# Seven multiplications instead of eight for some block products of the MLP, with groups of 1,024 columns

## The chip, the core and the metric

The kernel runs on one core of one Trainium2 chip. The metric is the device time of one execution in microseconds (us); before the change the median of 3 runs is 1461.17 us (1460.38 to 1461.81).

## What is computed

The reference is one layer of a decoder trunk on 256 tokens of width 2048, in float32. Three token mixers (softmax attention, gated linear attention, spatial gating) read one input projection, their outputs are merged by gates and projected by `w_o`; then comes the MLP, which is the part that the change touches:

```python
h = x + merged @ w_o
hn = rms_norm(h, n2)
return h + jnp.square(jax.nn.relu(hn @ w1)) @ w2     # w1: 2048 x 8192, w2: 8192 x 2048
```

## The kernel before

Every weight matrix is streamed from HBM once. A product in float32 is made of three matmuls: an operand is split into a rounded high part (type F32R) and the rest, and activation-high x weight-high, activation-high x weight-low and activation-low x weight-high are added up in PSUM. The activations are the stationary operand: `xT`, `yT`, `mT`, `hT` and `fT` hold them transposed, 16 k-tiles of 128 rows, high parts of the 256 tokens first, then the low parts. The weights are the moving operand.

`group_a` (L211) computes 512 output columns for both halves of the tokens (two PSUM banks, `ga`). It takes the weights in pieces from `weights` (L193): `fetch` (L170) brings 4 k-tiles x 512 columns, 1 MB, into `wraw` by one DMA on the SP queue (3 buffers); `split_w` (L182) makes the parts of two k-tiles, `whi` by a copy on ScalarE (L189) and `wlo` by a subtraction on VectorE (L190), 3 buffers each; `products` (L200) runs the 12 matmuls of such a piece (L207 to L209). After each piece `step` (L135) runs one waiting piece of other work, put there by `later` (L132).

The MLP goes through four phases `ph` of 2048 inner columns. In each, four groups with `w_ff1` on `hT` (L705) are followed by four with `w_ff2` on `fT` (L715). After a `w_ff1` group ScalarE applies ReLU and square (L708, L709) into `ft`, and `turn_into` (L649) turns `ft` back into `fT`: 4 transposes on TensorE into a bank `tt`, a copy on ScalarE for the high part, a subtraction on VectorE for the low one. One such step is called a turn here; there are two per 512 columns. After a `w_ff2` group VectorE adds the bank, scaled, to `h` (L718). `hT` is made the same way while `w_o` runs (L682 to L695), and its last two turns fall into the first group of the MLP. VectorE adds the `w_o` banks to `h` (L686) and ScalarE sums the squares of it (L688).

The order of the instructions is left to a scheduler, except for the first group of the kernel, where `tc.manual_schedule` keeps the written order on TensorE, ScalarE, VectorE and SP. Each engine works its own list in order.

Of the kernel before, what the change touches and what calls it, by code (L numbers as in the profile page):

```python
# [11 lines left out]
F32 = mybir.dt.float32  # L12
# [45 lines left out]
def trunk(ctx: ExitStack, tc: tile.TileContext, x, rpe_table, norm1_g, w_in, q_norm_g, k_norm_g,  # L58
# [24 lines left out]
    rows2 = cpool.tile([NV, P], F32, name="rows2")  # L83
# [4 lines left out]
    rpe = cpool.tile([NB, NH], F32, name="rpe")  # L88
    nc.gpsimd.dma_start(rpe, rpe_table)
    oneh = cpool.tile([NB, T], F32, name="oneh")  # L90
    nc.gpsimd.dma_start(oneh, onehot)
    lrwb = cpool.tile([LR + 1, 512], F32, name="lrwb")
    nc.gpsimd.dma_start(lrwb[:LR, :], gla_lr_w[0])
    nc.gpsimd.dma_start(lrwb[LR:LR + 1, :], gla_lr_b)
    og = cpool.tile([P, DV], F32, name="og")
    nc.gpsimd.dma_start(og, gla_out_g.to_broadcast([P, DV]))
    lng = cpool.tile([P, 512], F32, name="lng")
    nc.gpsimd.dma_start(lng, sg_ln_g.to_broadcast([P, 512]))
    lnb = cpool.tile([P, 512], F32, name="lnb")
    nc.gpsimd.dma_start(lnb, sg_ln_b.to_broadcast([P, 512]))  # L100
    sgw = cpool.tile([P, NH, P], F32, name="sgw")
    nc.gpsimd.dma_start(sgw, sg_w[0].rearrange("g t s -> t g s"))


    def tri(name, op, pat, cm):
        t = cpool.tile([P, P], F32, name=name)
# [10 lines left out]
    cum_r = cpool.tile([P, P], F32R, name="cum_r")  # L117
    nc.gpsimd.tensor_copy(cum_r, cum)
    rest_r = cpool.tile([P, P], F32R, name="rest_r")
    nc.gpsimd.tensor_copy(rest_r, rest)  # L120
    cind = cpool.tile([P, 2], F32, name="cind")
    nc.gpsimd.memset(cind, 0.0)
    nc.gpsimd.memset(cind[0:CH, 0:1], 1.0)
    nc.gpsimd.memset(cind[CH:P, 1:2], 1.0)
# [2 lines left out]
    def v3(t, a):  # L127
        return t.rearrange("p (a b) -> p a b", a=a)
# [116 lines left out]
    rb = gpool.tile([NB, NH, P], F32, name="rb")  # L245

    def first_group(c0):

# [43 lines left out]

    def squares(c):
        for tt in range(NT):
            junk = gpool.tile([P, XC], F32, tag="junk", name="junk")
# [109 lines left out]


    lrs = gpool.tile([P, NT, LR], F32, name="lrs")
    lrT = gpool.tile([LR + 1, T], F32, name="lrT")
    nc.vector.memset(lrT, 1.0)
    dec = gpool.tile([P, NT, NH, 2], F32, name="dec")  # L410
    G16 = 1.0 / 16.0
# [42 lines left out]
    wT = gpool.tile([P, NH, P], F32, name="wT")  # L454
    nc.gpsimd.memset(wT, 0.0)

    def w_turn():
# [130 lines left out]
    def outputs(hp, tt):  # L588
        if tt == 0:
            ob[hp] = v3(t4("ob"), NT)  # L590
        ps = bank("po")
        for j in range(2):
            hh = 2 * hp + j
            o = ps[:, j * DV:(j + 1) * DV]
            mm(o, am[:, tt, hh, :], vb[hp][:, tt, j * DV:(j + 1) * DV], start=True, stop=False, skip_group_check=True)  # L595
            for cc in range(2):
                c = 2 * tt + cc
                if c:
                    s = st[hp, 2] if c == 3 else st[hp, 0][:, c - 1, :]
                    mm(o[cc * CH:(cc + 1) * CH, :], qdT[:, hh, c * CH:(c + 1) * CH], s[:, j * DV:(j + 1) * DV],  # L600
                       start=False, stop=True, skip_group_check=True)
        nc.scalar.activation(ob[hp][:, tt, :], ps, AF.Copy)
        for j in range(2):
            junk = gpool.tile([P, XC], F32, tag="junk", name="junk")
# [49 lines left out]
    mg = None  # L654
    for n in range(D // 512):
        gts = []
        for i in range(3):
            pg = group_a(w_in[0], 0, KT, C_GATE + i * D + n * 512, 512, xT)
            if mg is None:
                drain()  # L660
                br_ctx.__exit__(None, None, None)
                mg = ctx.enter_context(tc.tile_pool(name="mg", bufs=1))
# [17 lines left out]
    hT = acts.tile([P, KT, 2 * T], F32R, tag="act0", name="hT")  # L680
    hsq = gpool.tile([P, NT, 4], F32, name="hsq")
    for n in range(D // 512):  # L682
        po = group_a(w_o[0], 0, KT, n * 512, 512, mT)
        for tt in range(NT):
            hv = h[:, tt, n * 512:(n + 1) * 512]
            nc.vector.tensor_add(hv, po[tt], hv)  # L686
            junk = gpool.tile([P, XC], F32, tag="junk", name="junk")
            nc.scalar.activation(junk, hv, AF.Square, accum_out=hsq[:, tt, n:n + 1])  # L688
        later()
        for jp in range(2):  # L690
            k = n * 4 + 2 * jp
            srcs = [h[:, tt, (k + j) * P:(k + j + 1) * P] for j in range(2) for tt in range(NT)]
            later(lambda k=k, srcs=srcs: turn_into(hT, k, srcs, V_N2))

    r2 = gpool.tile([P, NT], F32, name="r2")  # L695
    hs = gpool.tile([P, NT], F32, name="hs")
# [2 lines left out]
    nc.vector.reciprocal(r2, hs)  # L699


    fT = acts.tile([P, KT, 2 * T], F32R, tag="act1", name="fT")
    for ph in range(FF // D):
        for g in range(D // 512):
            pz = group_a(w_ff1[0], 0, KT, ph * D + g * 512, 512, hT)  # L705
            ft = mg.tile([P, NT, 512], F32, tag="ft", name="ft", bufs=2)
            for tt in range(NT):
                nc.scalar.activation(ft[:, tt, :], pz[tt], AF.Relu)  # L708
                nc.scalar.activation(ft[:, tt, :], ft[:, tt, :], AF.Square)  # L709
            later()  # L710
            for jp in range(2):
                srcs = [ft[:, tt, (2 * jp + j) * P:(2 * jp + j + 1) * P] for j in range(2) for tt in range(NT)]
                later(lambda k=g * 4 + 2 * jp, srcs=srcs: turn_into(fT, k, srcs, None))
        for n in range(D // 512):
            pf = group_a(w_ff2[0], ph * D, KT, n * 512, 512, fT)  # L715
            for tt in range(NT):
                hv = h[:, tt, n * 512:(n + 1) * 512]
                nc.vector.scalar_tensor_tensor(hv, pf[tt], r2[:, tt:tt + 1], hv, op0=ALU.mult, op1=ALU.add)  # L718
                if ph == FF // D - 1:
                    nc.sync.dma_start(out[0, tt * P:(tt + 1) * P, n * 512:(n + 1) * 512], hv)  # L720


# [20 lines left out]
```

## Time and profile before

| | us |
|---|---|
| median of 3 runs | 1461.17 |
| profiled execution | 1461.76 |
| its span | 1459.9 |
| TensorE busy | 1449.0 (99%) |
| VectorE busy | 758.7 (52%) |
| ScalarE busy | 685.1 (47%) |
| share of the 16 DMA engines, weight queue | 57.1% |

PE is TensorE's matmul row, PEld its weight load, DVE VectorE, ACT ScalarE, SP the queue that issues the DMAs. Matmuls are pipelined, so the time of one is read from the distance of two starts, not from its duration. The MLP runs from 743.07 us to the end.

### The profile page before, as it was taken

The numbers are of one execution on the slowest core, as the hardware profiler recorded it, in microseconds if no ns is written. First come the engines' busy times: TensorE is split into PE (matmuls) and PEld (weight loads), VectorE is DVE, ScalarE is ACT, GpSimd is POOL, SyncE is SP. The second block draws the span as 40 slices with busy tenths as digits, with TensorE's granted clock in tenths as the row PEclk, the third lists the DMA queues.
The fourth block names the chain that finished last, engine by engine and source line by source line (L and its number), as shares of the span: only waits on it lengthen the run. The fifth ranks groups of instructions, "written<-read, shape, count | busy, mean of one in ns | idle before, by whom it ended". The sixth has DMA issues, their size and how long they took to land.

```text
span 1459.9 us, 16296 instructions
## 1 busy us (share of the span) xinstructions
PE 1449.0 (99%) x6608; PEld 1197.8 (82%) x6608; DVE 758.7 (52%) x822; ACT 685.1 (47%) x821; POOL 14.0 (1%) x37
## 2 busy tenths in 40 slices
PE   8999999999999999999999999999999999999998
PEld 6899887788888888888888888888888888888887
DVE  5654655454645546465555455544544455554454
ACT  6457444454444444444545544445334554345432
POOL 2000000000000000000000000000000000000000
PEclk9999999999999999999999999999999999999999
DMA  8555554545655555555556555655556555666563
GB/s 281 185 183 163 182 177 137 181 155 191 201 180 195 195 185 196 193 185 183 188 173 187 188 188 189 199 177 198 181 194 201 175 193 182 200 189 186 181 222 115
DMA packets 138810, 272.19 MB, mean 186 GB/s; under 512 B 4748, under 2 KB 11440, under 8 KB 138736
## 3 DMA queue, kind: packets, MB, share of 16 engines
q1 hardware_dynamic: 137808, 268.59, 57.1%
q0 software_dynamic: 928, 2.57, 0.5%
q8 instruction: 51, 0.84, 0.2%
q14 instruction: 23, 0.19, 0.0%
HBM read 268.26 MB, written 2.88 MB: 186 GB/s over the span
## 4 chain that ended last, share of the span: by engine, by line
PE 99%; DMA 0%; SPq 0%; DVE 0%; issue 0%
PE ga L207 32%; PE ga L209 32%; PE ga L208 31%; PE tt L221 1%; PE pst L576 0%; DMA h<-in_x_dram 0%; PE po L600 0%; PE po L595 0%; PE qkt L221 0%; PE xt L221 0%; PE psc L364 0%; PE pbias L317 0%; PE pz L425 0%; PE pmx L465 0%; PE pam L557 0%; PE ybt L221 0%
## 5 line engine op out<-in xcount | busy, mean ns | idle before, releaser
L190 DVE TENSOR_TENSOR wlo<-wraw,whi 128x1024 fp32r<-128x1024 f32 (+3 forms) x520 | 619.2, 1193 | 644.3 <-ACT whi L189 644.1
L189 ACT ACTIVATE whi<-wraw 128x1024 fp32r<-128x1024 f32 (+3 forms) x520 | 537.8, 1036 | 720.8 <-PE ga L209 713.3
L207 PE MATMUL ga<-whi,xT 128*128 128x512 f32 (+2 forms) x768 | 297.8, 388 | 0.0
L208 PE MATMUL ga<-wlo,xT 128*128 128x512 f32 (+2 forms) x768 | 293.5, 382 | 0.0
L209 PE MATMUL ga<-whi,xT 128*128 128x512 f32 (+2 forms) x768 | 293.5, 382 | 0.0
L207 PE MATMUL ga<-whi,hT 128*128 128x512 f32 x512 | 201.7, 394 | 0.0
L207 PE MATMUL ga<-whi,fT 128*128 128x512 f32 x512 | 199.9, 391 | 0.0
L209 PE MATMUL ga<-whi,hT 128*128 128x512 f32 x512 | 199.5, 390 | 0.0
L209 PE MATMUL ga<-whi,fT 128*128 128x512 f32 x512 | 199.3, 389 | 0.0
L208 PE MATMUL ga<-wlo,fT 128*128 128x512 f32 x512 | 199.2, 389 | 0.0
L208 PE MATMUL ga<-wlo,hT 128*128 128x512 f32 x512 | 199.1, 389 | 0.0
L207 PEld LDWEIGHTS ga<-whi,xT 128*128 128x128 f32 x768 | 144.9, 189 | 29.8 <-issue 3.9
L209 PEld LDWEIGHTS ga<-whi,xT 128*128 128x128 f32 x768 | 144.7, 188 | 26.8
L208 PEld LDWEIGHTS ga<-wlo,xT 128*128 128x128 f32 x768 | 144.9, 189 | 25.2
L209 PEld LDWEIGHTS ga<-whi,hT 128*128 128x128 f32 x512 | 96.1, 188 | 20.3
L209 PEld LDWEIGHTS ga<-whi,fT 128*128 128x128 f32 x512 | 96.1, 188 | 20.0
L208 PEld LDWEIGHTS ga<-wlo,fT 128*128 128x128 f32 x512 | 96.2, 188 | 19.8
L207 PEld LDWEIGHTS ga<-whi,fT 128*128 128x128 f32 x512 | 96.1, 188 | 19.5
L208 PEld LDWEIGHTS ga<-wlo,hT 128*128 128x128 f32 x512 | 96.3, 188 | 19.2
L207 PEld LDWEIGHTS ga<-whi,hT 128*128 128x128 f32 x512 | 96.2, 188 | 19.0
L207 PE MATMUL ga<-whi,mT 128*128 128x512 f32 x128 | 51.4, 402 | 0.0
L209 PE MATMUL ga<-whi,mT 128*128 128x512 f32 x128 | 50.7, 396 | 0.0
(217 smaller groups left out, 825.0 us busy)
## 6 DMA issues: line engine op xcount, KB each, us to landing
wraw<-in_w_ff_dram SPq DMA_DIRECT2D x128, 1024.0 KB, 5.2
wraw<-in_w_in_dram SPq DMA_DIRECT2D x80, 1024.0 KB, 5.0
wraw<-in_w_o_dram SPq DMA_DIRECT2D x16, 1024.0 KB, 5.1
wraw<-in_w_br_b_dram SPq DMA_DIRECT2D x8, 1024.0 KB, 5.2
wraw<-in_w_in_dram SPq DMA_DIRECT2D x8, 692.0 KB, 4.1
wraw<-in_w_br_a_dram SPq DMA_DIRECT2D x4, 1024.0 KB, 5.2
wraw<-in_w_br_c_dram SPq DMA_DIRECT2D x4, 1024.0 KB, 5.1
wraw<-in_w_in_dram SPq DMA_DIRECT2D x6, 512.0 KB, 11.5
```

Source lines behind the costliest of these rows:

```text
L189: nc.scalar.activation(hi[:, j:j + per, :w], src, AF.Copy)
L190: nc.vector.tensor_tensor(lo[:, j:j + per, :w], src, hi[:, j:j + per, :w].bitcast(F32), ALU.subtract)
L207: mm(ps[tt][:, :w], xh, hi[:, j, :w], start=(k == 0), stop=False)
L208: mm(ps[tt][:, :w], xh, lo[:, j, :w], start=False, stop=False)
L209: mm(ps[tt][:, :w], xl, hi[:, j, :w], start=False, stop=(k == nk - 1))
L221: nc.tensor.transpose(ps[:, i * P:(i + 1) * P], s, ident)
```

## The change

The MLP now works in groups of 1,024 columns and takes the 16 k-tiles in 8 pairs. A pair of k-tiles, two halves of the tokens and two halves of the columns make a 2x2 block product. Five of the eight pairs ("P" in `ORDER = "PPSPSPSP"`) are computed with eight block multiplications as before (24 matmuls). The other three ("S") use a scheme with seven (21 matmuls): four sums of the weight blocks are formed on VectorE (`fsum`, L803 to L805), four sums of the activation blocks when the activations are turned (`sums`, L673 to L679), and at the end of a group the extra banks P1, P5, P6 and P7 are combined (`seven`, L831). An S pair is run as two pieces, "A" (3 products) and "B" (4). With the four output banks a group holds all 8 PSUM banks.

The weight pool, the gate pool and some small tiles now lie in memory that is given up before the MLP; the MLP's tiles (`fT`, `fraw`, `fhi`, `flo`, `fsum`, `fu`) lie in a pool of their own that is opened after the last `w_o` group. The whole MLP is written in a fixed order on TensorE, ScalarE, VectorE and SP: the parts of piece i+2 are prepared before the matmuls of piece i (`LEAD = 2`, three buffers), and the DMAs run two pairs ahead. L numbers in the diff's new functions are those of the changed kernel.

```diff
+ORDER = "PPSPSPSP"
+SEVEN = [i for i, c in enumerate(ORDER) if c == "S"]
...
-    def turn_into(dst, k, srcs, gain):
+    def turn_into(dst, k, srcs, gain, sums=None):
         ps = bank("tt")
         transpose4(ps, srcs)
-        split_ps(dst[:, k:k + 2, :], v3(ps, 2), None if gain is None else cols[:, gain + k:gain + k + 2])
+        if sums is not None:
+            a = scratch[-1].tile([P, 2, T], F32, tag="a32", name="a32")
+            if gain is None:
+                nc.scalar.activation(a, v3(ps, 2), AF.Copy)
...
+        split_ps(dst[:, k:k + 2, :], src, None if gain is None else cols[:, gain + k:gain + k + 2])
+        if sums is None:
+            return
+        b = src.rearrange("p j (t c) -> p (j t) c", c=P)
+        s = scratch[-1].tile([P, 4, P], F32, tag="s32", name="s32")
+        nc.vector.tensor_tensor(s[:, 0:2, :], b[:, 0:2, :], b[:, 1:4:2, :], ALU.subtract)
+        nc.vector.tensor_tensor(s[:, 2, :], s[:, 1, :], b[:, 0, :], ALU.subtract)
+        nc.vector.tensor_tensor(s[:, 3, :], s[:, 2, :], b[:, 2, :], ALU.add)
+        nc.scalar.activation(sums[:, 0], s, AF.Copy)
+        nc.vector.tensor_tensor(sums[:, 1], s, sums[:, 0].bitcast(F32), ALU.subtract)
...
+    mg_ctx.__exit__(None, None, None)
+    w_ctx.__exit__(None, None, None)
+    ffp = ctx.enter_context(tc.tile_pool(name="ffp", bufs=1, reuse_waits="tile"))
...
+    def prep(piece, raws):
+        g, what, kp, q = piece
+        raw = raws[q]
+        hi, lo = parts()
+        if what == "P":
+            split2(hi, lo, 0, 4, raw, 2 if q == 0 else 4)
+        elif what == "A":
+            ts = ffp.tile([P, 4, GW], F32, tag="fsum", name="fsum")
+            raws[q] = raw, ts
+            nc.vector.tensor_tensor(ts[:, 0:2], raw[:, 1:3], raw[:, 0:1].to_broadcast([P, 2, GW]), ALU.add)
+            nc.vector.tensor_add(ts[:, 2], ts[:, 0], raw[:, 2])
+            nc.vector.tensor_add(ts[:, 3], ts[:, 2], raw[:, 3])
+            split2(hi, lo, 0, 3, raw[:, 1:4])
+        else:
+            raw, ts = raws.pop(q)
+            split2(hi, lo, 0, 4, ts, 2)
+        return hi, lo
...
+            if what == "A":
+                todo = (("P1", block(g, kp, 0, 0)), ("c12", kind(g, kp, 3)), ("c11", block(g, kp, 0, 1)))
+            else:
+                todo = (("P5", kind(g, kp, 1)), ("P7", kind(g, kp, 0)), ("P6", kind(g, kp, 2)),
+                        ("c21", block(g, kp, 1, 1)))
+            for i, (role, a) in enumerate(todo):
+                g.three(role, *a, hi[:, i], lo[:, i])
+    def seven(g):
+        b = g.banks
+        u = ffp.tile([P, 4, GW], F32, tag="fu", name="fu")
+        nc.scalar.activation(u[:, 1], b["P1"], AF.Copy)
+        nc.vector.tensor_add(u[:, 0], u[:, 1], b["P6"])
+        nc.vector.tensor_add(u[:, 3], u[:, 0], b["P7"])
+        nc.vector.tensor_sub(u[:, 0], b["P5"], u[:, 0])
+        nc.vector.tensor_sub(u[:, 2], b["P5"], u[:, 3])
+        return u
...
+            nc.vector.tensor_add(u[:, 1], u[:, 1], b["c11"])
+            nc.vector.tensor_add(u[:, 3], u[:, 3], b["c21"])
+            nc.vector.tensor_add(u[:, 0], u[:, 0], b["c12"])
+            nc.vector.tensor_add(u[:, 2], u[:, 2], b["c22"])
+            for i in (1, 3, 0, 2):
+                nc.scalar.activation(u[:, i], u[:, i], AF.Relu)
+                nc.scalar.activation(u[:, i], u[:, i], AF.Square)
...
+    with tc.manual_schedule(engines=ORDERED):
+        for i in range(LEAD):
+            ready(i)
+        for i, piece in enumerate(pieces):
+            g = piece[0]
+            ends = i + 1 == len(pieces) or pieces[i + 1][0] is not g
+            if ends:
+                g.first(g)
+            ready(i + LEAD)
+            multiply(piece, wts.pop(i), half=turns.pop(0) if turns and len(turns) == 1 else None)
+            if len(turns) == 2:
+                turns.pop(0)()
+            step()
+            if ends:
+                turns = g.last(g)
```

`g.first` is `seven`, followed in a `w_ff2` group by four scaled additions into `h` (L869); `g.last` is the ReLU and square shown above (`w_ff1`) or four more such additions (`w_ff2`). A group of `w_ff1` leaves four turns, two after the first piece of the next group and two inside the second.

Two places of the order matter below. The first is VectorE after the end of a `w_ff1` group. Before, it goes on with weight parts (`wlo`) and two low parts of `fT`:

```order
L190 TENSOR_TENSOR wlo<-wraw,whi 128x1024 x7
L161 TENSOR_TENSOR fT<-tt,fT 128x2x256
L190 TENSOR_TENSOR wlo<-wraw,whi 128x1024
L161 TENSOR_TENSOR fT<-tt,fT 128x2x256
L190 TENSOR_TENSOR wlo<-wraw,whi 128x1024 x7
```

Now, after the end of the first `w_ff1` group (`flo` is the low part of a piece: 1536 wide for A, twice 1024 for B, 2048 for P; `a_5829`, `s_5833` and `sums` belong to a turn that also makes sums):

```order
L791 TENSOR_TENSOR flo<-fraw,fhi 128x1536
L166 TENSOR_TENSOR fT<-a_5829,fT 128x2x256
L675 TENSOR_TENSOR s_5833<-a_5829 128x256
L676 TENSOR_TENSOR s_5833<-s_5833,a_5829 128x128
L677 TENSOR_TENSOR s_5833<-s_5833,a_5829 128x128
L679 TENSOR_TENSOR sums<-s_5833,sums 128x512
L166 TENSOR_TENSOR fT<-tt,fT 128x2x256
L791 TENSOR_TENSOR flo<-fsum,fhi 128x1024 x2
L166 TENSOR_TENSOR fT<-tt,fT 128x2x256 x2
L791 TENSOR_TENSOR flo<-fraw,fhi 128x2048
```

The four turns stand between the low parts of the first A piece and of the first P piece behind it.

The second place is ScalarE where `w_o` ends and the MLP begins. Before (`whi` holds weights, `junk` the squares of the last `w_o` group), copies for the MLP stand on both sides of the squares:

```order
L189 ACTIVATE whi<-wraw 128x1024 x5
L688 ACTIVATE junk,hsq<-h 128x512 x2
L189 ACTIVATE whi<-wraw 128x1024 x2
L165 ACTIVATE hT<-tt,cols 128x256 x2
L189 ACTIVATE whi<-wraw 128x1024
```

Now (`fhi` holds weights of the MLP):

```order
L194 ACTIVATE whi<-wraw 128x1024 x2
L722 ACTIVATE junk,hsq<-h 128x512 x2
L790 ACTIVATE fhi<-fraw 128x1024 x2
L790 ACTIVATE fhi<-fraw 128x2048
L790 ACTIVATE fhi<-fraw 128x1536
L790 ACTIVATE fhi<-fsum 128x1024 x2
L664 ACTIVATE a_5547<-tt,cols 128x256 x2
L165 ACTIVATE hT<-a_5547 128x2x256
L678 ACTIVATE sums<-s_5552 128x512
L790 ACTIVATE fhi<-fraw 128x2048
```

All weight copies of the MLP have moved behind the squares, and the copy for the first P piece after an S pair stands behind a turn with sums.

## Rows read from the trace of the kernel before

**Rows 1.** The page: engines, and the chain that ended last by engine.

```profile
PE 1449.0 (99%) x6608; PEld 1197.8 (82%) x6608; DVE 758.7 (52%) x822; ACT 685.1 (47%) x821; POOL 14.0 (1%) x37
...
PE 99%; DMA 0%; SPq 0%; DVE 0%; issue 0%
```

**Rows 2.** Busy time by stretch, the MLP: engines, TensorE's granted clock, DMA share, GB/s.

```profile
755.00:1457.00 702.00, 700.46 (x3153) 579.99 (x3151) 346.95 (x315) 317.19 (x346) 0.00 (x0) 1.00 0.59 187
```

**Rows 3.** Instructions in time on TensorE, first MLP group: start, length, instruction.

```profile
744.68 0.39 PE L208 MATMUL ga<-wlo,hT 128*128 128x512 f32 x1
...
748.53 0.60 PE L221 MATMUL tt<-ident,h 128*128 128x128 f32 x4
...
749.20 0.39 PE L208 MATMUL ga<-wlo,hT 128*128 128x512 f32 x1
```

**Rows 4.** Groups by shape on VectorE: count | busy us, mean ns | idle before.

```profile
L190 DVE TENSOR_TENSOR wlo<-wraw,whi 128x1024 fp32r<-128x1024 f32 x480 | 587.8, 1225 | 621.9 <-ACT whi L189 621.7
L718 DVE SCALAR_TENSOR_TENSOR h<-ga,r,h 128x512 f32<-128x512 f32 x32 | 22.6, 744 | 5.1 <-PE ga L209 5.1
L161 DVE TENSOR_TENSOR fT<-tt,fT 128x512 fp32r<-128x512 f32 x32 | 21.9, 684 | 0.0
...
L167 DVE SCALAR_TENSOR_TENSOR hT<-tt,cols,hT 128x256 fp32r<-128x256 f32 x16 | 7.0, 477 | 0.0
...
L642 DVE TENSOR_TENSOR gate<-gate,og 128x256 f32<-128x256 f32 x8 | 2.8, 419 | 0.0
```

**Rows 5.** Groups by shape on ScalarE.

```profile
L189 ACT ACTIVATE whi<-wraw 128x1024 fp32r<-128x1024 f32 x480 | 509.7, 1062 | 704.9 <-PE ga L209 698.4 <-issue 4.7 <-DVE wlo L190 1.6
...
L165 ACT ACTIVATE hT<-tt,cols 128x256 fp32r<-128x256 f32 x16 | 6.6, 462 | 0.0
```

**Rows 6.** Instructions in time on VectorE, back to back (x2: two merged).

```profile
380.07 1.28 DVE L671 TENSOR_TENSOR gt<-ga,gt 128x512 f32<-128x512 f32 x2
381.27 1.28 DVE L673 TENSOR_TENSOR gt<-gt,gt 128x512 f32<-128x512 f32 x2
```

**Rows 7.** Instructions in time on ScalarE after a `w_ff1` group.

```profile
764.65 0.60 ACT L708 ACTIVATE ft<-ga 128x512 f32<-128x512 f32 x1 [0.30 <-PE ga L209]
765.28 0.63 ACT L709 ACTIVATE ft<-ft 128x512 f32<-128x512 f32 x1
...
766.50 1.05 ACT L189 ACTIVATE whi<-wraw 128x1024 fp32r<-128x1024 f32 x1
767.45 0.62 ACT L709 ACTIVATE ft<-ft 128x512 f32<-128x512 f32 x1
```

**Rows 8.** The same view of all engines, of ScalarE alone: the last `w_o` group.

```profile
742.70 1.28 DVE L686 TENSOR_TENSOR h<-ga,h 128x512 f32<-128x512 f32 x2
...
743.07 0.40 PE L207 MATMUL ga<-whi,hT 128*128 128x512 f32 x1
...
744.24 0.62 ACT L688 ACTIVATE junk<-h 128x512 f32<-128x512 f32 x1
...
745.51 0.19 ACT L688 ACTIVATION_READ_ACCUMULATOR junk<-h 128x1 f32 x1
```

**Rows 9.** DMA issues on the page: size, median us from issue to landing.

```profile
wraw<-in_w_ff_dram SPq DMA_DIRECT2D x128, 1024.0 KB, 5.2
```

**Rows 10.** Instructions in time on TensorE, the kernel's first weight matmuls.

```profile
9.01 0.63 PE L208 MATMUL ga<-wlo,xT 128*128 128x512 f32 x1
...
12.42 0.40 PE L207 MATMUL ga<-whi,xT 128*128 128x512 f32 x1
```

**Rows 11.** Groups by shape on TensorE.

```profile
L207 PE MATMUL ga<-whi,fT 128*128 128x512 f32 x512 | 199.9, 391 | 0.0
...
L207 PE MATMUL ga<-whi,mT 128*128 128x512 f32 x128 | 51.4, 402 | 0.0
```

**Rows 12.** Instructions in time at the very end.

```profile
1455.08 0.39 PE L209 MATMUL ga<-whi,fT 128*128 128x512 f32 x1
1455.50 0.75 DVE L718 SCALAR_TENSOR_TENSOR h<-ga,r,h 128x512 f32<-128x512 f32 x1 [0.61 <-PE ga L209]
```

More of the change, by code (lines that the diff above doesn't have):

```diff
@@ L646, in trunk @@
             later(lambda hp=hp, i=i: out_turn(hp, i))
-    def turn_into(dst, k, srcs, gain):
+    def turn_into(dst, k, srcs, gain, sums=None):
         ps = bank("tt")
         transpose4(ps, srcs)
-        split_ps(dst[:, k:k + 2, :], v3(ps, 2), None if gain is None else cols[:, gain + k:gain + k + 2])
-    mg = None
+        if sums is not None:
[3 more added lines that the diff above has]
+            else:
+                for j in range(2):
+                    nc.scalar.activation(a[:, j, :], v3(ps, 2)[:, j, :], AF.Copy,
+                                         scale=cols[:, gain + k + j:gain + k + j + 1])
+            src, gain = a, None
+        else:
+            src = v3(ps, 2)
+        split_ps(dst[:, k:k + 2, :], src, None if gain is None else cols[:, gain + k:gain + k + 2])
[8 more added lines that the diff above has]
+        nc.vector.tensor_tensor(sums[:, 1], s, sums[:, 0].bitcast(F32), ALU.subtract)
+    mg, scratch = None, []
     for n in range(D // 512):
@@ L661, in trunk @@
                 br_ctx.__exit__(None, None, None)
-                mg = ctx.enter_context(tc.tile_pool(name="mg", bufs=1))
+                early_ctx.__exit__(None, None, None)
+                mg_ctx = tc.tile_pool(name="mg", bufs=1)
+                mg = mg_ctx.__enter__()
+                scratch.append(mg)
                 mT = mg.tile([P, KT, 2 * T], F32R, name="mT")
@@ L680, in trunk @@
     hT = acts.tile([P, KT, 2 * T], F32R, tag="act0", name="hT")
+    sums = acts.tile([P, 2 * len(SEVEN), 2, 4, P], F32R, tag="act1", name="sums")
+    hS = {kp: sums[:, i] for i, kp in enumerate(SEVEN)}
+    fS = {kp: sums[:, len(SEVEN) + i] for i, kp in enumerate(SEVEN)}
     hsq = gpool.tile([P, NT, 4], F32, name="hsq")
@@ L699, in trunk @@
     nc.vector.reciprocal(r2, hs)
-    fT = acts.tile([P, KT, 2 * T], F32R, tag="act1", name="fT")
-    for ph in range(FF // D):
[L704 to L720, printed above, removed]
+    mg_ctx.__exit__(None, None, None)
@@ new lines, in trunk, with __init__, three @@
+    w_ctx.__exit__(None, None, None)
+    ffp = ctx.enter_context(tc.tile_pool(name="ffp", bufs=1, reuse_waits="tile"))
+    scratch.append(ffp)
+    fT = ffp.tile([P, KT, 2 * T], F32R, name="fT")
+    W2 = 2 * GW
+    class Group:
+        def __init__(self, src, r0, c0, act, sums, first, last):
+            self.src, self.r0, self.c0, self.act, self.sums = src, r0, c0, act, sums
+            self.first, self.last = first, last
+            self.banks, self.done = {}, {}
+            p, z = ORDER.count("P"), ORDER.count("S")
+            self.total = dict(c11=6 * p + 3 * z, c12=6 * p + 3 * z, c21=6 * p + 3 * z, c22=6 * p,
+                              P1=3 * z, P5=3 * z, P6=3 * z, P7=3 * z)
+        def three(self, role, ah, al, wh, wl):
+            if role not in self.banks:
+                self.banks[role], self.done[role] = bank(role), 0
+            for a, w in ((ah, wh), (ah, wl), (al, wh)):
+                n = self.done[role]
+                mm(self.banks[role], a, w, start=(n == 0), stop=(n == self.total[role] - 1))
+                self.done[role] = n + 1
@@ new lines, in block, with kind, fetch2 @@
+    def block(g, kp, tt, j):
+        k = 2 * kp + j
+        return g.act[:, k, tt * P:(tt + 1) * P], g.act[:, k, T + tt * P:T + (tt + 1) * P]
+    def kind(g, kp, i):
+        return g.sums[kp][:, 0, i, :], g.sums[kp][:, 1, i, :]
+    def fetch2(g, kp):
+        raw = ffp.tile([P, 2, W2], F32, tag="fraw", name="fraw", bufs=3)
+        nc.sync.dma_start(raw, g.src[g.r0 + 2 * kp * P:g.r0 + (2 * kp + 2) * P, g.c0:g.c0 + W2]
+                          .rearrange("(k p) c -> p k c", p=P))
+        return raw.rearrange("p k (c w) -> p (k c) w", c=2)
@@ new lines, in parts, with split2 @@
+    def parts():
+        return (ffp.tile([P, 4, GW], F32R, tag="fhi", name="fhi", bufs=3),
+                ffp.tile([P, 4, GW], F32R, tag="flo", name="flo", bufs=3))
+    def split2(hi, lo, a, b, src, step=4):
+        for i in range(a, b, step):
+            e = min(b, i + step)
+            nc.scalar.activation(hi[:, i:e], src[:, i - a:e - a], AF.Copy)
+            nc.vector.tensor_tensor(lo[:, i:e], src[:, i - a:e - a], hi[:, i:e].bitcast(F32), ALU.subtract)
+    def prep(piece, raws):
[11 more added lines that the diff above has]
+            split2(hi, lo, 0, 3, raw[:, 1:4])
+        else:
+            raw, ts = raws.pop(q)
+            split2(hi, lo, 0, 4, ts, 2)
+        return hi, lo
@@ new lines, in multiply @@
+    def multiply(piece, w, half=None):
+        g, what, kp, q = piece
+        hi, lo = w
+        if what == "P":
+            for tt in range(NT):
+                for j in range(2):
+                    for c in range(2):
+                        g.three(f"c{tt + 1}{2 - c}", *block(g, kp, tt, j), hi[:, 2 * j + c], lo[:, 2 * j + c])
+                if tt == 0 and half is not None:
+                    half()
+        else:
+            if what == "A":
+                todo = (("P1", block(g, kp, 0, 0)), ("c12", kind(g, kp, 3)), ("c11", block(g, kp, 0, 1)))
+            else:
+                todo = (("P5", kind(g, kp, 1)), ("P7", kind(g, kp, 0)), ("P6", kind(g, kp, 2)),
+                        ("c21", block(g, kp, 1, 1)))
+            for i, (role, a) in enumerate(todo):
+                g.three(role, *a, hi[:, i], lo[:, i])
@@ new lines, in seven, with square_in, first, last @@
+    def seven(g):
[7 more added lines that the diff above has]
+        return u
+    def square_in(ph, n):
+        def first(g):
+            g.u = seven(g)
+        def last(g):
+            b, u = g.banks, g.u
+            nc.vector.tensor_add(u[:, 1], u[:, 1], b["c11"])
[5 more added lines that the diff above has]
+                nc.scalar.activation(u[:, i], u[:, i], AF.Square)
+            def turns(c):
+                for jp in range(2):
+                    k = n * 8 + c * 4 + 2 * jp
+                    srcs = [u[:, 2 * tt + c, (2 * jp + j) * P:(2 * jp + j + 1) * P] for j in range(2) for tt in range(NT)]
+                    turn_into(fT, k, srcs, None, fS.get(k // 2))
+            return [lambda: turns(1), lambda: turns(0)]
+        return first, last
@@ new lines, in add_in, with into, first, last @@
+    def add_in(ph, n):
+        def into(tt, c, src):
+            hv = h[:, tt, n * W2 + c * GW:n * W2 + (c + 1) * GW]
+            nc.vector.scalar_tensor_tensor(hv, src, r2[:, tt:tt + 1], hv, op0=ALU.mult, op1=ALU.add)
+            return hv
+        def first(g):
+            u = seven(g)
+            for tt, c in ((0, 1), (1, 1), (0, 0), (1, 0)):
+                into(tt, c, u[:, 2 * tt + c])
+        def last(g):
+            for tt in range(NT):
+                for c in range(2):
+                    hv = into(tt, c, g.banks[f"c{tt + 1}{2 - c}"])
+                    if ph == FF // D - 1:
+                        c0 = n * W2 + c * GW
+                        nc.sync.dma_start(out[0, tt * P:(tt + 1) * P, c0:c0 + GW], hv)
+            return []
+        return first, last
@@ new lines, in trunk @@
+    groups = []
+    for ph in range(FF // D):
+        for n in range(2):
+            groups.append(Group(w_ff1[0], 0, ph * D + n * W2, hT, hS, *square_in(ph, n)))
+        for n in range(2):
+            groups.append(Group(w_ff2[0], ph * D, n * W2, fT, fS, *add_in(ph, n)))
+    pieces, quads = [], []
+    for g in groups:
+        for kp, c in enumerate(ORDER):
+            pieces += [(g, w, kp, len(quads)) for w in ("P" if c == "P" else "AB")]
+            quads.append((g, kp))
+    raws, wts, turns = {}, {}, []
@@ new lines, in trunk, with ready @@
+    LEAD = 2
+    def ready(i):
+        if i < len(pieces):
+            q = pieces[i][3]
+            while len(fetched) < min(q + 3, len(quads)):
+                raws[len(fetched)] = fetch2(*quads[len(fetched)])
+                fetched.append(1)
+            wts[i] = prep(pieces[i], raws)
+    fetched = []
+    with tc.manual_schedule(engines=ORDERED):
[13 more added lines that the diff above has]
+                turns = g.last(g)
```

45 lines of the change are left out of this document (24 added, 21 removed).

## The prediction, made before the changed kernel had run

> **What bounds the kernel now.** I read the page first. TensorE is busy 99% of the span and the chain that ended last is 99% TensorE [rows 1]. In the MLP it is the same: 700.46 of 702.00 us, with VectorE busy 347 us (49%) and ScalarE 317 us (45%) [rows 2]. So a matmul that goes away shortens the kernel, as long as the other engines keep feeding TensorE. The price of a matmul comes from its starts: from 744.68 to 748.53 us stand 17 intervals, 0.2265 us each, although each record is 0.39 us long. A turn and one matmul take 749.20 - 748.53 = 0.67 us, so the turn's transposes cost 0.44 us [rows 3]. As a check: 3072 matmuls x 0.2265 + 34 turns x 0.44 = 710.8 us, and the MLP's matmuls take 1455.3 - 743.1 = 712.2 us.
>
> **What is saved.** A P pair costs 24 matmuls, an S pair 21. With 16 groups of 5 P and 3 S there are 16 x (120 + 63) = 2928 instead of 3072. The turns stay. 144 x 0.2265 = **32.6 us less** on TensorE. The matmuls now change their PSUM bank after 3 instead of 6; the 17 intervals above span such changes and show no cost, so I add none (bounds 0 and 0).
>
> **What VectorE and ScalarE must do for it.** VectorE's subtraction costs 0.684 us for 512 columns and 1.225 for 1024 [rows 4]; the line through both gives 1.77 for 1536 and 2.31 for 2048. ScalarE's copies cost 1.062 for 1024 [rows 5] and 0.63 for 512 [rows 7], so 1.50 and 1.93. The 256-wide VectorE operation takes 0.42 [rows 4]; its 128-wide sums are on the same line, 0.28. An S pair then holds VectorE for 1.225 + 2 x 0.684 (sums) + 1.77 + 2 x 1.225 (low parts) = 6.81 us while TensorE needs only 21 x 0.2265 = 4.76. A P pair is 2.31 against 5.44. Per cycle "P, A, B" that is 9.1 against 10.2 us: VectorE goes from half busy to about nine tenths.
>
> How tightly operations follow each other matters now. Two independent ones start 1.20 us apart per pair of 512 columns (380.07, 381.27), 0.60 each: 0.085 less than their length [rows 6]. ScalarE gives back 0.10 (766.50 + 1.05 against 767.45), but an operation that reads the one just before it starts 0.03 after its end (764.65 + 0.60 against 765.28) [rows 7]. I use these three, and 0.03 us for a hand-over between engines.
>
> The Trainium skill ("VectorE: DVE Perf Modes", the section on the DRAIN) says that the next VectorE operation does not start until the pipe of the one before is empty. Rows 6 show starts 0.085 us before the end; what full lengths would cost is the second rival below.
>
> **Inside a group the cycle holds.** Piece i+2 uses the buffers of piece i-1. So a P piece's parts start when the P piece before it has ended: the last matmul's record ends 0.16 us after its slot, then 1.93 (ScalarE) and 2.31 (VectorE) with hand-overs, 4.5 us. TensorE meanwhile runs A and B, 21 matmuls and the first of P: 4.98 us. Margin 0.5 us. VectorE is then about 1 us idle per cycle. Cost 0; if it were 0.3 us short, 48 cycles x 0.3 = 14 us, as an upper bound.
>
> **The end of a w_ff1 group does not hold.** I count from the start of the group's last A piece. VectorE: low part of the last P until 4.5, low part of the next group's first P until 6.7, four combinations of `seven` (three of them dependent) until 9.2, the second P until 11.4. Then the four additions; the first ends at 12.0, the last at 13.8. ScalarE squares: ReLU and square, four times 0.63 + 0.03 + 0.63 - 0.10, from 12.05 to 16.9. Only then, in its list, comes the high part of the first A piece: 18.35. VectorE's low part ends at 20.15. Now the turns, in which the two engines wait for each other: copy and high part on ScalarE until 19.5, low part and sums on VectorE until 21.7, high part of the sums 22.4, of the next turn 22.9. Then the two halves of B, 23.85 and 24.8 (low parts until 26.25), the last two turns on ScalarE until 25.8, and the first P piece behind it: high part 27.7, low part **30.0**. TensorE's supply until then is 2 + 2.7 + 3 x 5.44 + 4 x 0.44 + 2 + 2.7 = 27.6, and its second matmul wants the low part at 27.85. It stands still for **2.2 us**. After the second `w_ff1` group of a phase one more turn makes sums: copy, dependent copy, three sums and high part add 3.15 us to the same chain, so **5.4 us**. Four phases: 4 x 7.6 = **30.5 us**. Bounds: 15 us if every link were shorter by a tenth of a microsecond (some 10 links count), 45 with full lengths.
>
> At the end of a `w_ff2` group there is no ScalarE work, only eight additions of 0.744 [rows 4]. The same count gives the A piece's low part 0.4 us before TensorE wants it. Cost 0, bounds 0 and 7 x 1 us.
>
> **The start of the MLP.** Before, ScalarE and VectorE had the first MLP weights ready when `w_o` ended, and the first `hT` matmul starts without a gap at 743.07 [rows 8]. Now these copies stand behind the squares of the last `w_o` group. The first addition ends at about 743.4 [rows 8], the squares take 745.70 - 744.24 = 1.46 us, so they end at 744.9. High part of the first half 1.06, low part 1.23: the second matmul starts at 747.25 instead of 743.3, the piece ends at 752.5. The second weight DMA lands in memory that these squares use: 744.9 + 5.2 [rows 9] + 1.93 + 2.31 = 754.4, the second piece ends at 759.6, with its turn 760.1. A and its turn, P5 and P7 run until 763.9. P6 needs the bank of the last turn, and VectorE reads that bank only behind the sums of the other turn and the next P piece's low part: 760.2 + copies 1.5 (two of 0.462 [rows 5], one of 0.63) + low part and sums 1.75 + 0.65 + 1.93 + 2.31 + two of 0.477 [rows 4] = 769.1. The B piece ends at 770.5 instead of 759.6: **10.9 us**. Bounds: 9 (DMA lands 2 us earlier) and 14 (the next gap's slow matmuls, below).
>
> **The tail.** Before, VectorE ends 0.95 us after the last matmul slot (1456.25 against 1455.3) [rows 12]. Now eight scaled additions and four combinations stand there and end about 3.2 us after it: **2.2 us** (bounds 1.4 and 3).
>
> **Two things I put at nothing.** `w_o`: its matmuls' records are 402 ns against 391 for `fT` [rows 11]; `mT` has moved in memory, so 384 matmuls may gain 0.007 each (-2.6 us), or those of `fT`, moved next to the weights, may lose as much (1464 x 0.007 = 10 us). The sums in two `w_o` turns hide under a VectorE that is half idle (0 to 1 us). DMA: as many bytes and requests of 1 MB, issued two pairs, some 10 us, ahead of a landing time of 5.2 us.
>
> **Sum.** -32.6 + 30.5 + 10.9 + 2.2 = +11.0 on the profiled 1461.76, which lies 0.6 above the median: **1472 us**.
>
> **Rivals.**
> *The vector engines run ahead.* By sums, a `w_ff1` group wants 42 us of VectorE less 5 of overlap, and TensorE 43: it fits, and if the work spreads, the group ends cost nothing. Then 1461.2 - 32.6 + 10.9 + 2.2 = 1442. It decides at the first P piece after a group's start: ready by 27.85 us or not. Against it: three buffers allow two pieces of lead, and the fixed order puts turns ahead of that piece. Chance 0.17, with all that keeps over half of the stalls away (up to 1458).
> *Slower links or a slower clock.* With full lengths on VectorE each `w_ff1` end costs some 0.8 us more and each `w_ff2` end 1.0: 8 x 0.8 + 7 x 1.0 = 13, so 1485. The clock: the kernel's first matmuls, after an idle start, stand 0.426 us apart (9.01 to 12.42, 8 intervals) [rows 10], which is the 1.2 GHz level, though the granted clock of that stretch reads 1.00; then 0.2265. Nine such matmuls cost 1.8 us. If each of nine gaps (eight group ends, the start) brought that, 16 us: 1488. "TensorE: Matmul & The Clock Gate" of the Trainium skill has the array fall to half clock after idling; no row of this MLP has a gap to show it. The gaps here are mostly shorter than the kernel's idle start. Chance 0.19 for 1481 and more.
> *Gain and cost cancel*, within 0.2% (1458.2 to 1464.1, about what a measurement of this kernel can tell from no change), chance 0.12.
>
> **Numbers.** The forecast, 1464 to 1481, has the remaining 0.52. Faster by over 0.2%: 0.17, within: 0.12, slower: 0.71. The range 1452 to 1489 leaves out most of the first rival and little above.
>
> **What would show it.** Right: 2928 MLP matmuls still 0.2265 apart; VectorE near 85 to 90% in the MLP; TensorE idle some 11 us around 743 to 771, about 2 us at the first P piece after an S pair behind the first `w_ff1` group of a phase and about 5 behind the second, released by VectorE's `flo`; none behind `w_ff2` groups. Wrong: no idle time there (first rival), or idle in every cycle, or matmuls 0.23 and more apart in stretches without idle.

## The result, and the profile after

The changed kernel takes **1495.39 us** (median of 4 runs, 1494.45 to 1497.89) against 1461.16 before: ratio 1.0237, 95% interval 1.0219 to 1.0255. It is slower, as forecast, but by 34 us instead of 11, and outside the range of 1452 to 1489. The profiled execution has a span of 1493.3 us.

The page (engines, and the chain that ended last, by engine) answers to [rows 1]:

```profile
PE 1452.7 (97%) x6464; PEld 1172.1 (78%) x6464; DVE 1042.3 (70%) x1120; ACT 762.9 (51%) x836; POOL 13.9 (1%) x37
...
PE 83%; DVE 8%; ACT 6%; issue 3%; DMA 1%; SPq 0%; DVEq 0%; ACTq 0%
```

TensorE executes 144 matmuls less, yet its busy time has not fallen (1449.0 before). That is the first sign: each matmul must take more time. The second sign is the chain, of which TensorE has only 83% now.

Busy time by stretch (columns as in [rows 2]): 100 us of a stage that the change does not touch, and the MLP.

```profile
400.00:500.00 100.00, 100.00 (x437) 80.25 (x436) 51.35 (x50) 42.33 (x44) 0.00 (x0) 1.00 0.57 187
...
759.50:1487.00 727.50, 701.53 (x3063) 565.12 (x3064) 634.05 (x613) 400.14 (x366) 0.00 (x0) 0.99 0.54 185
```

The same 100 us of the kernel before hold 447 matmuls:

```profile
400.00:500.00 100.00, 100.00 (x447) 82.84 (x446) 51.27 (x49) 44.92 (x47) 0.00 (x0) 1.00 0.58 192
```

So the unchanged `xT` stage is 2% slower, without any idle time, at a full granted clock. Instructions in time on TensorE there: after the change, 15 intervals between these two,

```profile
401.71 0.39 PE L213 MATMUL ga<-wlo,xT 128*128 128x512 f32 x1
...
405.21 0.39 PE L213 MATMUL ga<-wlo,xT 128*128 128x512 f32 x1
```

3.50 / 15 = 0.2333 us each; before, 21 intervals from 400.10 to 404.86,

```profile
400.10 0.39 PE L209 MATMUL ga<-whi,xT 128*128 128x512 f32 x1
...
404.86 0.39 PE L209 MATMUL ga<-whi,xT 128*128 128x512 f32 x1
```

4.76 / 21 = 0.2267 us. The record is 0.39 us long in both: only the distance of starts shows it.

What TensorE waited for, and for how long (total, times, longest):

```profile
PE P L767 <- DVE fT L166: 14.0, 8, 3.0
PE c L767 <- DVE flo L791: 6.9, 9, 1.4
PE P L767 <- DVE hT L172: 5.0, 1, 5.0
...
PE c L767 <- ACT fhi L790: 2.5, 1, 2.5
```

Adding up the distances between all starts on TensorE (under 0.26 us: a matmul at its pace, against 0.227; above: a wait), the two traces differ by these terms. Their sum is the whole difference of the spans, 1493.3 - 1459.9 = 33.4 us:

| term | forecast, us | measured, us |
|---|---|---|
| 144 matmuls fewer | -32.6 | -32.7 |
| waits in and at the start of the MLP, with matmuls at half clock behind them | +41.4 | +36.7 |
| tail after the last matmul | +2.2 | +1.4 |
| transposes, other | 0 | +1.4 |
| **pace of matmuls that do not wait** | **0** | **+26.6** (14.0 ahead of the MLP, 12.6 in it) |

### The profile page after: what moved, and what is told of

Same layout as the page of the kernel before. It is cut to its first block, busy times and chain, and to the rows that moved or that the text cites. A ratio compares the mean times of both kernels' runs of the same rounds, so it can differ in the third digit from the quotient of the medians.

```text
span 1493.3 us, 16287 instructions
## 1 busy us (share of the span) xinstructions
PE 1452.7 (97%) x6464; PEld 1172.1 (78%) x6464; DVE 1042.3 (70%) x1120; ACT 762.9 (51%) x836; POOL 13.9 (1%) x37
## 4 chain that ended last, share of the span: by engine, by line
PE 83%; DVE 8%; ACT 6%; issue 3%; DMA 1%; SPq 0%; DVEq 0%; ACTq 0%
PE c L767 25%; PE ga L212 16%; PE ga L214 16%; PE ga L213 16%; PE P L767 7%; DVE flo L791 4%; ACT fhi L790 3%; ACT fu L854 1%; ACT fu L855 1%; ACT fT L165 1%; DVE fT L166 1%; PE tt L226 0%; PE pst L581 0%; DVE fu L837 0%; DVE fu L839 0%
## 5 line engine op out<-in xcount | busy, mean ns | idle before, releaser
L195 DVE TENSOR_TENSOR wlo<-wraw,whi 128x1024 fp32r<-128x1024 f32 (+3 forms) x264 | 305.4, 1161 | 298.1 <-ACT whi L194 297.8
L194 ACT ACTIVATE whi<-wraw 128x1024 fp32r<-128x1024 f32 (+3 forms) x264 | 265.1, 1008 | 352.3 <-PE ga L214 346.5
L791 DVE TENSOR_TENSOR flo<-fraw,fhi 128x2048 fp32r<-128x2048 f32 (+2 forms) x129 | 266.1, 2073 | 77.2 <-ACT fhi L790 76.9
L790 ACT ACTIVATE fhi<-fraw 128x2048 fp32r<-128x2048 f32 (+2 forms) x129 | 224.0, 1744 | 126.2 <-PE c L767 112.5
L767 PE MATMUL c<-fhi,hT 128*128 128x512 f32 x736 | 242.0, 396 | 2.5 <-ACT fhi L790 2.5
L767 PE MATMUL c<-fhi,fT 128*128 128x512 f32 x736 | 239.5, 393 | 0.0
L767 PEld LDWEIGHTS c<-fhi,hT 128*128 128x128 f32 x736 | 138.7, 188 | 36.6 <-ACT fhi L790 3.0
L767 PEld LDWEIGHTS c<-fhi,fT 128*128 128x128 f32 x736 | 139.2, 189 | 30.4
L767 PE MATMUL c<-flo,hT 128*128 128x512 f32 x368 | 146.7, 399 | 3.7 <-DVE flo L791 3.7
L767 PE MATMUL c<-flo,fT 128*128 128x512 f32 x368 | 145.2, 395 | 3.2 <-DVE flo L791 3.2
```

Of the source, the lines that this page charges most:

```text
L194: nc.scalar.activation(hi[:, j:j + per, :w], src, AF.Copy)
L195: nc.vector.tensor_tensor(lo[:, j:j + per, :w], src, hi[:, j:j + per, :w].bitcast(F32), ALU.subtract)
L767: mm(self.banks[role], a, w, start=(n == 0), stop=(n == self.total[role] - 1))
L790: nc.scalar.activation(hi[:, i:e], src[:, i - a:e - a], AF.Copy)
L791: nc.vector.tensor_tensor(lo[:, i:e], src[:, i - a:e - a], hi[:, i:e].bitcast(F32), ALU.subtract)
```

## The experiments

### The pace

Ahead of the turns of `w_o` the instructions are the same in both kernels; the buffers lie elsewhere, because the pools were rearranged. My first theory was **placement**: the pace depends on where the moving operand (weights) and the stationary one (activations) start, modulo 128 bytes. Rivals: busier VectorE and ScalarE take something from TensorE's reads; weights at the far end of memory (right side) are slower. Offsets below are bytes within a partition; they follow from the order and the sizes of the program's tiles, and the trace does not show them.

```diff
     yT = acts.tile([P, KT, 2 * T], F32R, tag="act1", name="yT")
+    acts.tile([P, 16], F32, tag="pad", name="pad")
```

> The kernel before with one unused tile of 64 bytes per partition between the activations and the weight buffers: same instructions, all weights 64 bytes further. Start addresses within 128 bytes: moving weights 32, stationary xT, yT, hT, fT 96 (equal before), mT 0. Placement theory (a matmul of 512 columns takes 227 ns where both operands start at the same place within 128 bytes, 233.4 where not): 5472 matmuls lose 6.3 ns each, +34 us, about 1495 us, and matmuls 231 to 238 ns apart everywhere. Vector-traffic theory (busier VectorE and ScalarE slow TensorE's reads) and right-side theory (weights at the far end of memory): no change, 1461 us.

Measured: 1472.38 us (ratio 1.0079, 1.0066 to 1.0093). An unused tile makes the kernel 11 us slower, with the same instructions: traffic and right side fall as the whole cause. But the size is a third of the forecast: matmuls stand 229.1 ns apart (`xT`, `hT`), not 233, and the stretch holds 442 of them:

```profile
400.00:500.00 100.00, 100.00 (x442) 82.10 (x441) 51.14 (x48) 43.82 (x47) 0.00 (x0) 1.00 0.57 189
```

The same with 32 elements (128 bytes):

> The same with a tile of 128 bytes: the weights start 128 bytes further, at the same place within 128 bytes as before (96 and 96). Placement theory with a period of 128 bytes: no change, 1461 us within 0.2%. If the period is longer (256 or more): as with 64 bytes, about 1495 us. The other theories: 1461 us.

Measured: 1493.41 us (1.0221, 1.0207 to 1.0235). Busy time by stretch, as above:

```profile
400.00:500.00 100.00, 100.00 (x439) 81.11 (x437) 50.51 (x48) 43.15 (x45) 0.00 (x0) 1.00 0.55 183
```

439 matmuls instead of 447: with operands at equal places within 128 bytes all stages are slow. The period of 128 bytes is wrong. Two more kernels rested on that period and missed too. `mT` moved by 32 bytes:

```diff
+                mg.tile([P, 8], F32, name="pad")
                 mT = mg.tile([P, KT, 2 * T], F32R, name="mT")
```

> The kernel before with an unused tile of 32 bytes ahead of mT, which brings mT from 64 to 96 within 128 bytes, where whi and wlo start. Placement theory: the 384 matmuls of w_o gain 6.6 ns each, -2.6 us, about 1458.5 us, and the w_o matmuls stand 227 ns apart. Vector-traffic and right-side theories: no change, 1461.2 us, w_o at 234 ns.

Measured: 1462.4 us (1.0006, 0.9997 to 1.0015), `w_o` still at 233.3 ns. And the changed kernel aligned at 128 bytes:

```diff
+    acts.tile([P, 16], F32, name="pad0")
+    gpool.tile([P, 8], F32, name="pad1")
     xT = acts.tile([P, KT, 2 * T], F32R, tag="act0", name="xT")
```

> The changed kernel with unused tiles of 64 bytes ahead of the activations and 32 bytes at the end of the small tiles: every moving and stationary operand of a 512-column matmul then starts at 96 within 128 bytes (before this edit 32 against 96 for xT and yT, 0 against 96 for mT, 32 against 0 for hT and the sums, 0 against 0 for fT). Nothing else changes. Placement theory: 2400 x 6.3 + 384 x 6.5 + 1752 x 6.4 ns = 28.9 us less matmul time, of which some 3 us come back as longer stalls, since the vector engines' chains at the group ends stay as long: about 1469 us. Vector-traffic theory and right-side theory: no change, 1495 us.

Measured: 1493.8 us (1.0229, 1.0215 to 1.0243 against before). `xT`, `yT`, `hT` and the sums stayed at 232.6 to 233.1 ns; `mT` and `fT` came to 227.7 and 227.5. Set side by side, the stages of these runs follow one rule: fast where both operands start at the same place within **256** bytes. The second theory has that period. `mT` by 160 bytes (`mg.tile([P, 40], ...)`):

> The kernel before with an unused tile of 160 bytes ahead of mT: mT then starts at 96 within 256 bytes, as whi and wlo do (before 192). Placement theory with a period of 256 bytes, formed on the runs so far (fast in every stage whose two operands start at the same place within 256 bytes, slow in every other): 384 matmuls gain 6.9 ns each, -2.6 us, about 1458.5 us, w_o at 227 ns. If placement acts in another way: no change, 1461.1 us.

Measured: **1458.87 us** (0.9984, 0.9975 to 0.9993); forecast 1458.5. Groups on TensorE, `w_o`'s first products:

```profile
L207 PE MATMUL ga<-whi,mT 128*128 128x512 f32 x128 | 50.6, 395 | 0.0
```

against 402 ns in [rows 11]; the starts stand 227.4 ns apart instead of 234.0. Three more tiles between activations and weights, of 256, 32 and 192 bytes:

> The same with 256 bytes: start addresses differ from the kernel before, places within 256 bytes do not. Placement theory with a period of 256 bytes: 227 ns and 1461 us, no change. With a longer period (512 bytes or more): slower, towards 1494 us.

Measured: 1461.38 us (1.0000, 0.9990 to 1.0011), and 447 matmuls again in the stretch:

```profile
400.00:500.00 100.00, 100.00 (x447) 82.81 (x446) 51.48 (x49) 45.01 (x47) 0.00 (x0) 1.00 0.58 191
```

> The kernel before with an unused tile of 32 bytes between the activations and the weights: moving operands start 32 bytes behind the stationary ones within 256 bytes (before: 0). Placement theory with a price that grows with the distance (0: 227.0 ns, 64: 229.1): about 228 ns, 5088 x 1.0 = +5 us, 1466 us. If any distance that is not 0 costs at least as much as 64 bytes do: 1472 us or more.

Measured: 1495.21 us (1.0234, 1.0213 to 1.0254). The expected growth with distance is refuted; even 32 bytes cost the full price:

```profile
400.00:500.00 100.00, 100.00 (x436) 80.45 (x435) 51.41 (x50) 42.39 (x44) 0.00 (x0) 1.00 0.57 187
```

> The same with 192 bytes: moving operands start 192 bytes behind the stationary ones, or 64 ahead. If the price depends on the distance in either direction: as with 64 bytes, about 229 ns and 1472 us. If it depends on the direction (distances of 96 to 160 cost 233 to 234 ns): 233 ns or more, about 1494 us.

Measured: 1494.62 us (1.0230, 1.0209 to 1.0249), 233.3 ns. So 64 bytes ahead cost what other distances cost, and 64 behind is the only cheaper one seen. By start of the weights minus start of the activations, within 256 bytes (mean distance of starts in stages whose matmuls all have that distance):

| bytes | 0 | 32 | 64 | 96 | 128 | 160 | 192 |
|---|---|---|---|---|---|---|---|
| ns | 226.7 to 227.7 | 233.3 | 228.9 to 229.1 | 233.3 to 233.7 | 232.6 to 233.3 | 234.0 to 234.2 | 233.3 |

Then the changed kernel with everything at the same place (192 bytes ahead of the activations, 160 behind the small tiles):

> The changed kernel with unused tiles of 192 bytes ahead of the activations and 160 bytes at the end of the small tiles: every operand of a 512-column matmul starts at 224 within 256 bytes. Nothing else changes. Placement theory (256 bytes): 2400 x 6.3 + 384 x 6.3 + 1752 x 6.3 ns = 28.6 us less matmul time, some 3 us of it given back as longer stalls, about 1470 us; all matmul groups at 227 to 228 ns. Vector-traffic theory: pre-MLP groups may become fast, but hT and sums stay at 233 because VectorE is 90% busy there: about 1481 us.

Measured: 1479.48 us (1.0120, 1.0106 to 1.0134 against before), 15.9 less than the changed kernel, where 25 were expected. By the distances of starts the pace did what was forecast: 29.4 us of excess over 227 ns became 0.9, so -28.5. Nine matmuls with sums in a row, in the changed kernel (1.87 / 8 = 0.234 us each) and here (1.81 / 8 = 0.226):

```profile
888.76 0.39 PE L767 MATMUL P<-fhi,sums 128*128 128x512 f32 x1
...
890.63 0.39 PE L767 MATMUL P<-fhi,sums 128*128 128x512 f32 x1
...
875.14 0.39 PE L769 MATMUL P<-fhi,sums 128*128 128x512 f32 x1
...
876.95 0.39 PE L769 MATMUL P<-fhi,sums 128*128 128x512 f32 x1
```

The rivals fall for good: `hT` and the sums run at 227 ns beside a VectorE as busy as before (87% of the MLP), with the weights ahead of the MLP still on the right side. By its time alone (1481 forecast by the vector-traffic theory) this run would have fitted the wrong theory; the distances of starts tell them apart. The rest was given back. Waits (first row) grew by 4.0 us, most likely since TensorE now comes sooner to the same late links, and more matmuls of the MLP ran at half clock (55 distances of 0.42 to 0.43 us instead of 15: +8.0):

```profile
PE P L769 <- DVE fT L166: 17.1, 8, 3.3
```

Busy time by stretch behind one such wait, with the granted clock third from the end (0.53, so most of it at the 1.2 GHz level):

```profile
863.20:870.40 7.20, 6.31 (x17) 4.46 (x16) 7.11 (x6) 3.48 (x3) 0.00 (x0) 0.53 0.44 146
```

### The waits

Here is the changed kernel's end of a second `w_ff1` group, instructions in time on TensorE:

```profile
874.32 0.39 PE L767 MATMUL P<-fhi,sums 128*128 128x512 f32 x1
877.71 0.50 PE L767 MATMUL P<-fhi,sums 128*128 128x512 f32 x1 [3.00 <-DVE fT L166]
...
878.70 0.63 PE L767 MATMUL c<-fhi,fT 128*128 128x512 f32 x1
879.13 0.63 PE L767 MATMUL c<-flo,fT 128*128 128x512 f32 x1
...
880.99 0.80 PE L767 MATMUL c<-flo,fT 128*128 128x512 f32 x1 [0.38 <-DVE flo L791]
```

P6 waits 3.0 us for the bank of the last turn, which VectorE's low part of `fT` sets free; then the next P piece waits for its low part. Between them matmuls start 0.43 us apart: half clock. The busy time by stretch shows it there (granted clock 0.50, the 1.2 GHz level) and, at the same place one phase later, not (1.00), although P6 waited 3.0 us both times:

```profile
878.40:881.60 3.20, 2.82 (x8) 1.71 (x7) 2.96 (x2) 1.58 (x2) 0.00 (x0) 0.50 0.00 0
1057.40:1060.40 3.00, 1.81 (x7) 1.16 (x7) 2.13 (x1) 2.21 (x2) 0.00 (x0) 1.00 0.00 0
```

One phase later, on VectorE and ScalarE:

```profile
1043.82 0.63 ACT L855 ACTIVATE fu<-fu 128x512 f32<-128x512 f32 x1
1044.36 1.47 ACT L790 ACTIVATE fhi<-fraw 128x1536 fp32r<-128x1536 f32 x1
...
1045.86 1.76 DVE L791 TENSOR_TENSOR flo<-fraw,fhi 128x1536 fp32r<-128x1536 f32 x1 [1.91 <-ACT fhi L790]
...
1055.98 0.69 DVE L679 TENSOR_TENSOR sums<-s,sums 128x512 fp32r<-128x512 f32 x1 [0.70 <-ACT sums L678]
1056.59 0.68 DVE L166 TENSOR_TENSOR fT<-tt,fT 128x512 fp32r<-128x512 f32 x1
1058.27 2.29 DVE L791 TENSOR_TENSOR flo<-fraw,fhi 128x2048 fp32r<-128x2048 f32 x1 [0.99 <-ACT fhi L790]
```

VectorE, 87% busy in the MLP, stands idle here for 1.91, 0.70 and 0.99 us, each time for ScalarE. If that order causes the waits, another order removes them with the same work. On top of the aligned kernel:

```diff
-            return [lambda: turns(1), lambda: turns(0)]
+            return [relu_square, lambda: turns(1), lambda: turns(0)]
...
             ready(i + LEAD)
+            while deferred:
+                deferred.pop()()
+            if len(turns) == 3:
+                turns.pop(0)()
             multiply(piece, wts.pop(i), half=turns.pop(0) if turns and len(turns) == 1 else None)
```

`relu_square` holds the eight ScalarE operations that stood in `last`; `deferred` holds the high and low part of a turn's sums; a new `turn_two` does both turns of a pair, the one without sums first.

> The kernel of the run before (aligned at 256 bytes) with the vector engines' fixed order changed at the ends of the w_ff1 groups alone: ReLU and squares behind the next A piece's high part, the turn without sums first, a turn's sums split behind the next piece's parts. Chain theory (the stalls at group ends come from the order of a chain between VectorE and ScalarE, 1.5 us after the first w_ff1 group of a phase and 4.9 after the second, and two of four half-clock stretches follow from them): 25.8 + 3 us go, about 1442 us. Throughput theory (VectorE has too much work around the group ends, whatever the order): the waits come back at the next P piece, about 1470 us. Half and half: 1456 us.

Measured: **1439.47 us** (0.9853, 0.9840 to 0.9867 against before). That is 40.0 us less than the aligned kernel, more than the waits I had counted in the changed kernel, since both they and the half clock had grown there. Each engine runs as many instructions as before, so the order brought it; the edit changes it in three places at once, and what each of them is worth was not measured. Of the MLP's waits the ones at the start are left:

```profile
PE P L769 <- DVE hT L172: 5.1, 1, 5.1
...
PE c L769 <- ACT fhi L792: 2.5, 1, 2.5
...
PE c L769 <- DVE flo L793: 0.8, 1, 0.8
```

Then the start: the last `w_o` group's additions, squares and turns are written out behind the first two pieces' parts.

```diff
         for i in range(LEAD):
             ready(i)
+        c0 = D - 512
+        for tt in range(NT):
+            nc.vector.tensor_add(h[:, tt, c0:], po[tt], h[:, tt, c0:])
...
+        turns = [lambda: None, last_turns, last_squares]
```

> The kernel of the run before, with the start of the MLP changed too: the first two pieces' weight parts come ahead of the last w_o group's additions and squares on VectorE and ScalarE, the last two hT turns one piece earlier and the squares behind them. Chain theory: the waits at the start, 2.7 + 1.0 + 1.3 + 5.2 + 0.3 = 10.5 us, and one half-clock stretch of 1.7 us go but for some 1 us, about 1431 us, below the kernel before. If the weights' first transfers are what is late: 4 us stay, 1435 us.

Measured: **1427.33 us** (0.9767, 0.9752 to 0.9782): 2.3% faster than the kernel before, and 4 us less than forecast. The MLP by stretch:

```profile
741.00:1420.00 679.00, 678.99 (x3064) 563.03 (x3062) 629.95 (x617) 398.04 (x367) 0.00 (x0) 1.00 0.57 194
```

TensorE never stands still, beside a VectorE that is 629.95 / 679.00 = 93% busy. So the vector engines do have the throughput, and they do not slow a matmul: `hT`, sums and `fT` stand 226.8 to 226.9 ns apart.

Last, the aligned kernel with eight P pairs, ends and start not mended (`ORDER = "PPPPPPPP"`, no sums, no combinations):

> The changed kernel, aligned at 256 bytes, with all eight pairs as P: no block product with seven multiplications and no sums; the 1,024-column groups, the fixed order and the start of the MLP stay, ends and start not mended. 3072 matmuls. Chain theory (stalls at the group ends come from the sums, the combinations and the additions that the S pairs bring): no stall at the ends, some 5 us of waits at the start with a half-clock stretch of 2 to 3 us, w_o 2.6 us faster than in the kernel before: about 1465 us. If the 1,024-column groups in fixed order cause the stalls themselves: 25 us more, about 1490 us.

Measured: 1464.8 us (1.0028, 1.0017 to 1.0039). Only the start's waits are there (2.5 and 0.8 us); the ends cost nothing. What the ends cost comes with the S pairs, not with groups of 1,024 columns in a fixed order. This run takes away the work of the S pairs too, so it does not tell an order from a lack of throughput; the run with the ends mended does.

## Why the prediction was wrong

**The step that failed is "Two things I put at nothing".** It saw that `mT`'s matmuls differ from `fT`'s by 0.007 us and that memory placement could be why. It then priced only `w_o` (-2.6) and `fT` (+10), and put both at nothing. The size per matmul was right; what carries it was wrong. It is not the place of one buffer but the distance between two, and the change moved all buffers: `xT` and `yT` (now at a distance of 192 bytes) and `hT` (96) lost the equality with the weights within 256 bytes that they had before, the sums, which are new, lie at 96, `fT` kept the equality, and `w_o` went from one slow distance (160) to another (96). That is 26.6 us; the other terms together came out 4 us below the forecast. The rule came only from the runs, but a bound could have been had before: [rows 11] already held one slow pair, with 160 bytes between `mT` and the weights, and fast ones with 0, and the addresses that would change follow from the pools. "Matmuls 0.23 and more apart in stretches without idle" stood among the signs of being wrong, and it is the sign that came.

The Trainium skill ("SBUF — State Buffer", the section on who interferes with whom) gives TensorE's moving operand and weight load independent read ports and says that TensorE never waits on anyone. The rows agree for other engines (93% busy VectorE, 226.8 ns), and not between TensorE's own two operands (436 or 447 matmuls in the same 100 us, by where the two start). Whether the reads are what waits there, no run shows.

**What is saved** was right: -32.7, and the version without waits keeps it: 1427.33 against 1458.87 for the kernel before with `mT` aligned is -31.5.

**Inside a group the cycle holds**: right; no waits there.

**The end of a `w_ff1` group**: 2.2 and 5.4 us forecast; 1.5 and about 5.0 measured. The place was half right. More of it is the wait of P6 for a turn's bank (14.0 us in all) than the P piece's low part (5.0; the other 1.9 of that row's 6.9 us fall into the start), because the chain is late already when the turn's own low part comes. The theory behind it, an order and not a lack of throughput, stands by the run with the ends mended.

**The start**: 10.9 forecast; 2.7 + 1.0 + 1.3 + 5.2 and small ones, 10.5, measured, with the wait for P6's bank where it was said. (Two sums of the working are off in the last digit, 769.1 for 769.3 and 30.5 for 4 x 7.6; nothing hangs on them.)

**The tail**: 2.2 forecast, 1.4 measured:

```profile
1486.67 2.72 DVE L869 SCALAR_TENSOR_TENSOR h<-c,r,h 128x512 f32<-128x512 f32 x4
...
1487.04 0.39 PE L767 MATMUL c<-fhi,fT 128*128 128x512 f32 x1
```

**The rivals.** Slower VectorE links: no, the ends were shorter than forecast. The slower clock: in part. Half clock (matmuls 0.43 us apart, granted clock 0.50, the 1.2 GHz level) follows the wait of 5.0 us at the start and two of the four second ends, and not the first ends, whose waits are under 0.7 us. P6 waited 3.0 us at all four second ends, so the length of that wait alone does not tell the two from the others. It costs some 3 us here, not 16; some 11 in the aligned kernel. The Trainium skill ("TensorE: Matmul & The Clock Gate", the section on HAM oscillation) warns of just this behind gaps in TensorE's work; the trace agrees, at a smaller price than I gave the rival. Vector engines that run ahead: no, though a mended order brings what that rival hoped for.

## What to carry to other kernels

Before any change that moves buffers, list the start addresses of both matmul operands within 256 bytes, and pad until they are equal: for these 128x512 fp32r matmuls that is worth 3% of each (227 against 233 ns), and it costs an unused tile. When an unchanged stage gets slower, compare distances of starts, not record lengths. Where VectorE is close to full, write its order so that it never waits for the other engine in a chain: 40 and then 12 us were won here with the same work.

## What the runs showed of the hardware

- The pace of a 128x512 fp32r matmul depends on the distance between its operands' start addresses within 256 bytes: 227 ns at 0, 229 at 64, 232.6 to 234.2 at the other five distances tried. A distance of 224 was not tried, and why 64 is cheaper, and what inside the chip has this period, stay open.
- Which stationary operand counts, that of the matmul itself or the next one that is loaded, stays open. Where stages mix, `fT` (distance 0) and sums, the slow pace spreads: at a distance of 96 for the sums (changed kernel) the 48 intervals from an `fT` matmul to a sums matmul are 234.6 ns on average and the 46 from sums to `fT` 229.2; at 128 (changed kernel aligned at 128 bytes) 233.7 and 234.2, both slow. `fT` to `fT` is 228.2 ns in the changed kernel, where such changes stand between, and 226.8 in the kernel before.
- At half clock matmuls start 0.43 us apart. The MLP of the changed kernel has three such stretches, that of the aligned kernel six. P6's waits at the second ends are 3.0 us in the one, two of four followed by half clock, and 3.3 in the other, all four followed by it; why two of the first four were not is open.
